# The dilation-16 attention group by 16 classes of 64 tokens, in 64x64 products

## The chip, the cores and the metric

The kernel runs on one core of a Trainium2 chip. The metric is the device time of one execution in microseconds, the median over the runs shown. Inside the core, TensorE (PE) multiplies matrices and writes to PSUM, PEld is its weight load, VectorE (DVE), ScalarE (ACT) and GpSimd (POOL) work element by element, and SyncE (SP) and POOL issue DMAs between HBM and SBUF.

## The reference, cut to what matters

A residual stream of 1024 tokens by 1024 channels goes through two layers. Layer 0 is a gated short convolution (a product 1024 to 8192 columns, a width-3 convolution, a product 2048 to 1024). Layer 1 is dilated attention:

```python
proj = h @ w_in                                   # 3 groups x (q, k, v) x 16 heads x 64, and z
for g, (window, dilation) in enumerate(((128, 1), (512, 4), (2048, 16))):
    q = rms_norm(qkv[:, :, g, 0], q_gain[g]); k = rms_norm(qkv[:, :, g, 1], k_gain[g])
    # query t sees keys t - dilation*j, j = 0..128, causal, plus a bias of the distance
    o, l = dilated_group_attention(q, k, v, bias_g, window, dilation)
alpha = softmax(stack(lses)); o = sum(alpha * outs)   # the groups are merged by their denominators
y = o * silu(z); x = x + y @ w_out
```

With dilation 16 the 1024 tokens fall into 16 residue classes of 64 tokens. Within a class, attention is plain causal attention over 64 positions; tokens of different classes don't see each other.

## The kernel before, in words

All tensors are float32, and channels lie on partitions (two heads of 64 on 128 partitions). The program has three stages in time.

**Convolution** (to about 790 us) and **projections** (to about 1624 us). Both multiply by a Strassen scheme in three-term split products of 128x128 by 512 (lines L301 to L304), so PE does one of these every 0.23 us. The order of PE's instructions is written out by hand; the other engines' order comes from a planner that estimates times. Weights are loaded by SP, mixed on POOL (L276) and split on ACT and DVE (L164, L165). The projections come in pairs of 128 columns, one pair for q and k (`qk`), then one of v for two units (`v`), then the gate (`z`). A unit is a pair of heads `hp` (8 of them) and a group `g` (0, 1, 2 for dilation 1, 4, 16).

For a `qk` pair, `norm` computes the RMS norm two pairs later: for each half `hf` of the tokens and each of q and k, DVE multiplies the raw product by the gain and the row factor (L711) and writes it into a scratch half tile with the tokens sorted by residue class (1, 4 or 8 classes; `c`), and POOL stores each half tile to HBM (`qkd`, L716). For a `v` pair, `got` scales the product into scratch (POOL at L683 for three of four pieces, DVE at L681 for the fourth); `turn` then transposes it in 128-token blocks (PE, L727; `blk` picks the tokens of a block, for dilation 16 every eighth token) and stores it (`vd`, L733).

**Attention** (1624 to 1972 us). All engines' orders are written by hand: `attention(hp, g)` makes steps, and a loop takes one step per iteration: part A of step k, part C of step k-4, then the later parts of the merging, then part B of step k-2, and then, in iterations 33 to 48, 53 to 68 and from 73 on, one piece of the output projection ("dense", L1091 to L1093). A unit of group 0 or 1 has 4 steps, a unit of group 2 has 2, so a head pair takes 10 iterations.

For dilation 16 the kernel treats the tokens as 8 classes of dilation 8, each one block of 128 tokens. Half of each 128x128 score block belongs to the other residue modulo 16, and the bias table masks it.
- A: 4 blocks x 2 heads of 64x128 products `q x k` into two score banks (L902); then, per block and head, DVE adds the bias and takes the row maximum (L919, with a read of the accumulator), and ACT takes the exponential and its row sum (L922).
- B: PE transposes the 8 blocks (L929), and ACT or DVE copies them out of PSUM (L859, L857).
- C: per block, head and query half, a product of V (128 keys) with the transposed weights (L942), written with a step of 8 tokens into two output banks; after the second step `finish` copies them to SBUF (DVE, L959).

Merging of the three groups: `store` writes the row maxima and sums of groups 0 and 1 to HBM (`nld`) and, at group 2, loads them back (`ml`, L965, on POOL's queue). `weights` (DVE, L979 and on) and `shares` (to L997) make the shares; `store_shares` (L1000) writes them and `spread` (L1005) loads them back broadcast. For the last head pair `spread_last` does this with PE transposes instead (L1040: 24 for each token half), and `last` multiplies (L1047).

SP loads q and k (L831), v (L839), bias tables (L872) and others some iterations ahead. DMA waits are in order on each queue.

## Time and profile before

| what | value |
|---|---|
| median of 3 runs | 1978.61 us (1975.02 to 1979.72) |
| the profiled execution | 1973.57 us, span 1971.8 us |
| PE busy | 1925.4 us, 98% of the span |
| DVE busy | 1493.2 us, 76% |
| ACT busy | 903.5 us, 46% |
| POOL busy | 880.9 us, 45% |
| chain that ended last | PE 78%, DVE 12%, issue 4%, DMA 4%, ACT 3% |

Busy times are shares of the whole span, over stages with different limits. A busy PE is one with a matmul in flight; several small ones can be in flight at once, so what a stretch of small products costs is read from the start of one run of instructions to the start of the next.

### The profile page before, as it was taken

What the parts mean: (1) busy time and instruction counts of PE and PEld (TensorE: products, weight loads), DVE (VectorE), ACT (ScalarE), POOL (GpSimd) and SP (SyncE); (2) the same over time, 40 slices, a digit from 0 to 9 for tenths busy, and PEclk for the clock granted to TensorE, in tenths of its full rate; (3) what the DMA queues carried; (4) which work ended last, traced back from release to release, by engine and by line L of the source; (5) the groups of instructions that cost most, each with busy time, mean ns of one, the idle gap of its engine ahead of it and who ended that gap; (6) DMA issues with size and microseconds to landing.
All of it is one profiled execution on the core that took longest, in us unless ns stands there. A gap on an engine that the chain in (4) does not pass through costs nothing.

```text
span 1971.8 us, 30228 instructions
## 1 busy us (share of the span) xinstructions
PE 1925.4 (98%) x10654; PEld 1566.2 (79%) x10654; DVE 1493.2 (76%) x2754; ACT 903.5 (46%) x2042; POOL 880.9 (45%) x800
## 2 busy tenths in 40 slices
PE   8999999999999999999999999999999999899998
PEld 6888888888888888878888888788888876677777
DVE  7866666666566555788889689968998866788886
ACT  6433333333334454444333443434334339877781
POOL 0366657666665211344445445444444451323230
PEclk9999999999999999999999999999999999999999
DMA  5312232222224575423233233324333257978752
GB/s 195 118 58 91 83 107 76 96 89 84 91 70 152 185 239 167 133 76 112 103 118 118 76 118 106 118 76 128 87 107 107 98 180 248 258 222 225 203 158 86
DMA packets 116807, 254.28 MB, mean 129 GB/s; under 512 B 15822, under 2 KB 22718, under 8 KB 116656
## 3 DMA queue, kind: packets, MB, share of 16 engines
q1 hardware_dynamic: 93024, 177.42, 28.3%
q0 software_dynamic: 23632, 74.95, 12.6%
q8 instruction: 83, 1.36, 0.3%
q14 instruction: 68, 0.56, 0.1%
HBM read 193.05 MB, written 67.64 MB: 132 GB/s over the span
## 4 chain that ended last, share of the span: by engine, by line
PE 78%; DVE 12%; issue 4%; DMA 4%; ACT 3%; SPq 0%; POOL 0%; DVEq 0%; POOLq 0%; ACTq 0%
PE pp L301 18%; PE pp L304 18%; PE pp L303 18%; PE pp L552 3%; PE pp L553 3%; PE pp L551 3%; DVE ws L165 2%; PE pt L929 2%; DVE blkc L711 1%; PE pp L374 1%; PE po L948 1%; PE pp L375 1%; PE pp L376 1%; ACT xs L922 1%; DMA wraw<-in_wo 1%
## 5 line engine op out<-in xcount | busy, mean ns | idle before, releaser
L165 DVE TENSOR_TENSOR ws<-wr,ws 128x512 fp32r<-128x512 f32 x284 | 281.2, 992 | 115.5 <-ACT ws L164 113.9
L164 ACT ACTIVATE ws<-wr 128x512 fp32r<-128x512 f32 x284 | 178.3, 630 | 361.3 <-PE pp L304 238.9
L164 ACT ACTIVATE ws<-sr 128x512 fp32r<-128x512 f32 x272 | 169.9, 629 | 294.0 <-PE pp L304 244.1
L276 POOL TENSOR_TENSOR sr<-wr 128x512 f32<-128x512 f32 x136 | 185.0, 1360 | 261.1 <-DMA wr<-in_wqk 74.8
L165 DVE TENSOR_TENSOR ws<-sr,ws 128x512 fp32r<-128x512 f32 x272 | 228.7, 848 | 74.0 <-ACT ws L164 71.4
L313 DVE TENSOR_TENSOR f<-pp,f 128x512 f32<-128x512 f32 x204 | 139.7, 685 | 91.3 <-PE pp L304 84.3
L922 ACT ACTIVATE xs<-xs,nl 128x128 f32<-128x128 f32 (+1 forms) x384 | 167.9, 440 | 49.6 <-DVE nl L919 48.0
L309 ACT ACTIVATE f<-pp 128x512 f32<-128x512 f32 x228 | 132.5, 581 | 26.3 <-POOL blkc L683 12.2
L716 POOL DMA_DIRECT2D qkd<-blkc x96 | 68.0, 716 | 133.8 <-DVE blkc L711 126.4
L919 DVE CUSTOM_DVE_ANT_0 xs<-ps,bt 128x128 f32<-128x128 f32 (+1 forms) x384 | 110.7, 347 | 21.3 <-PE ps L907 14.3
L674 ACT ACTIVATE f<-f 128x512 f32<-128x512 f32 x96 | 60.7, 632 | 142.0 <-DVE f L313 104.8
L276 POOL TENSOR_TENSOR sr<-wr,sr 128x512 f32<-128x512 f32 x68 | 88.8, 1305 | 67.2 <-issue 43.9
L301 PE MATMUL pp<-blkg,ws 128*128 128x512 f32 x272 | 107.0, 393 | 3.4 <-ACT f L309 3.4
L301 PE MATMUL pp<-blkf,ws 128*128 128x512 f32 x272 | 108.5, 399 | 0.7 <-ACT f L309 0.7
L301 PE MATMUL pp<-blka,ws 128*128 128x512 f32 x272 | 107.1, 394 | 0.7 <-ACT f L309 0.7
L301 PE MATMUL pp<-blkb,ws 128*128 128x512 f32 x272 | 107.4, 395 | 0.0
L301 PE MATMUL pp<-blkd,ws 128*128 128x512 f32 x272 | 107.0, 393 | 0.0
L304 PE MATMUL pp<-blkf,ws 128*128 128x512 f32 x272 | 106.3, 391 | 0.0
L304 PE MATMUL pp<-blkd,ws 128*128 128x512 f32 x272 | 106.0, 390 | 0.0
L304 PE MATMUL pp<-blka,ws 128*128 128x512 f32 x272 | 106.0, 390 | 0.0
L304 PE MATMUL pp<-blkb,ws 128*128 128x512 f32 x272 | 106.0, 390 | 0.0
L303 PE MATMUL pp<-blkg,ws 128*128 128x512 f32 x272 | 105.9, 389 | 0.0
(335 smaller groups left out, 5356.6 us busy)
## 6 DMA issues: line engine op xcount, KB each, us to landing
wr<-in_conv_w_in SPq DMA_DIRECT2D x128, 256.0 KB, 3.1
wr<-in_wqk SPq DMA_DIRECT2D x96, 256.0 KB, 3.1
qkd<-blkc POOLq DMA_DIRECT2D x96, 256.0 KB, 3.2
qk<-qkd SPq DMA_DIRECT2D x48, 512.0 KB, 6.5
wr<-in_conv_w_out SPq DMA_DIRECT2D x64, 256.0 KB, 3.1
f<-in_x SPq DMA_DIRECT2D x48, 256.0 KB, 4.1
wr<-in_wv SPq DMA_DIRECT2D x48, 256.0 KB, 3.0
vd<-f POOLq DMA_DIRECT2D x48, 256.0 KB, 2.5
```

What stands on the lines that cost most here:

```text
L164: nc.scalar.activation(t[:, 0], src, AF.Copy)
L165: nc.vector.tensor_tensor(t[:, 1], src, t[:, 0].bitcast(F32), op=OP.subtract)
L276: nc.gpsimd.tensor_tensor(t, x, y, op=op)
L301: nc.tensor.matmul(ps, w[:, 0, ws], b[:, k, 0], start=new and k == 0, stop=False, skip_group_check=not new)
L303: nc.tensor.matmul(ps, w[:, 0, ws], b[:, k, 1], start=False, stop=False, skip_group_check=not new)
L304: nc.tensor.matmul(ps, w[:, 1, ws], b[:, k, 0], start=False, stop=end and k == 3, skip_group_check=not new)
L309: nc.scalar.activation(t, ps, AF.Copy)
L313: nc.vector.tensor_tensor(m, ps, m, op=OP.add)
L674: nc.scalar.activation(sq, t, AF.Square)
L716: nc.gpsimd.dma_start(qkd[hp, g, which].rearrange("p (c s) -> p c s", c=c) [:, :, hf * m:(hf + 1) * m], o.rearrange("p (c s) -> p c s", c=c))
L919: nc.vector.tensor_tensor_reduce(out=x, in0=ps[s][:, x0:x0 + nk].rearrange("p a b -> p (a b)"), in1=u["bt"][s][:, bs], op0=OP.add, op1=OP. ...
L922: nc.scalar.activation(x, x, AF.Exp, bias=nm, scale=-1.0, accum_out=L)
```

## The change

Group 2 is treated as 16 classes of 64 tokens. Scores and values become 64x64 products: each uses one quarter of PE (64 rows by 64 columns), and four consecutive ones use the four quarters. A step of group 2 takes 8 classes: in A 16 products write scores of 128 partitions (two classes) by 64 keys, so DVE and ACT run over 64 columns in place of 128; in B two classes side by side share one transpose, 4 in place of 8; in C 16 products of 64x64.

What goes with it: `norm` sorts group 2 into 16 classes and writes whole 1024-token tiles, stored by one DMA for q and one for k (2 per unit in place of 4); `got` writes group 2's v sorted by class; `turn` then reads contiguous blocks; the bias of group 2 is loaded as 64 rows twice; `finish` sorts the output back to token order while it copies; `ml` and `store_shares` become two DMAs of 64 partitions each; `spread_last` uses products with a 64-column selection of the identity in place of transposes; the bias table of group 2 has no masked half.

```diff
@@ got, kind v
-                        if ps is not None:
-                            nc.vector.tensor_tensor(vt, ps, R1[:, cs], op=OP.mult)
-                        else:
-                            nc.gpsimd.tensor_tensor(vt, t, R1[:, cs], op=OP.mult)
+                        eng, t, r = (nc.vector, ps, R1[:, cs]) if ps is not None else (nc.gpsimd, t, R1[:, cs])
+                        if units[p[1] + col][1] == 2:
+                            vt = spare()[:, col * S:col * S + S].rearrange("p (r x i) -> p i x r", r=4, x=4)
+                            vt = vt[:, hf * 32:hf * 32 + 32]
+                            t, r = (y.rearrange("p (i x r) -> p i x r", x=4, r=4) for y in (t, r))
+                        eng.tensor_tensor(vt, t, r, op=OP.mult)
@@ norm
-                            nc.gpsimd.dma_start(qkd[hp, g, which].rearrange("p (c s) -> p c s", c=c)
-                                                [:, :, hf * m:(hf + 1) * m], o.rearrange("p (c s) -> p c s", c=c))
+                    for which in range(2):
+                        nc.gpsimd.dma_start(qkd[hp, g, which], out_tile(which))
@@ prefetch
+                    if g == 2:
+                        for hs in (lo, up):
+                            nc.sync.dma_start(b0[hs, :64], rows[:64, :64])
@@ A
+                    for n, j in enumerate(js) if g == 2 else ():
+                        for h in range(2):
+                            cols = slice((8 * h + j) * 64, (8 * h + j) * 64 + 64)
+                            for s, hs in enumerate((lo, up)):
+                                nc.tensor.matmul(flat[s][64 * h:64 * h + 64, n * 64:n * 64 + 64], q[hs, cols],
+                                                 k[hs, cols], start=True, stop=True)
+                        todo.append((slice(n * 64, n * 64 + 64), j, slice(0, 64)))
+                        if n % 2 == 0:
+                            c.append((n // 2, j, 2 * j, True, True))
@@ C
-                            if g == 2:
-                                for q in range(2):
-                                    nc.tensor.matmul(u["po", q][hs].rearrange("p (i r) -> p r i", r=8)[:, j],
-                                                     V[:, vb, hs], pts[s][:, i, q * 64:q * 64 + 64], start=f, stop=l)
+                        for a in range(2) if g == 2 else ():
+                            for s, hs in enumerate((lo, up)):
+                                for h in range(2):
+                                    rows = slice(64 * h, 64 * h + 64)
+                                    nc.tensor.matmul(u["po", h][hs, (vb + a) * 64:(vb + a) * 64 + 64],
+                                                     V[rows, vb + a, hs], pts[s][rows, i, 64 * a:64 * a + 64],
+                                                     start=True, stop=True)
@@ finish
+                if g == 2:
+                    nc.vector.tensor_copy(O[hp, g].rearrange("p (i a h r) -> p h r a i", a=2, h=2, r=4)[:, q],
+                                          u["po", q].rearrange("p (r a i) -> p r a i", r=4, a=2))
@@ store, store_shares
-                    nc.gpsimd.dma_start(u["ml"], nld[hp].rearrange("(i r) g e -> i r g e", r=8))
+                    for a, hs in enumerate((lo, up)):
+                        nc.gpsimd.dma_start(u["ml"][hs], nld[hp].rearrange("(i a r) g e -> a i r g e", a=2, r=8)[a])
-                nc.gpsimd.dma_start(fd[hp].rearrange("w s (i r) -> i w s r", r=8), u["fo"])
+                for a, hs in enumerate((lo, up)):
+                    nc.gpsimd.dma_start(fd[hp].rearrange("w s (i a r) -> a i w s r", a=2, r=8)[a], u["fo"][hs])
@@ spread_last
-                        nc.tensor.transpose(fb.rearrange("p (i r) -> p r i", r=8)[:, r],
-                                            u["wide", w][hs, r * P:r * P + P], ident[hs, hs])
+                        nc.tensor.matmul(fb.rearrange("p (i a r) -> p r a i", a=2, r=8)[:, r],
+                                         u["wide", w][:, r * P:r * P + P], mine, start=True, stop=True)
```

## Rows read from the trace of the kernel before

**Rows 1.** The head of the profile's page: the span, and of each engine the busy time, its share of the span and the number of instructions.
```profile
span 1971.8 us, 30228 instructions
PE 1925.4 (98%) x10654; PEld 1566.2 (79%) x10654; DVE 1493.2 (76%) x2754; ACT 903.5 (46%) x2042; POOL 880.9 (45%) x800
```

**Rows 2.** Busy time by stretch. The columns are the stretch (us), its length, the busy time of PE, PEld, DVE, ACT and POOL with the number of instructions, the granted TensorE clock, the share of time that the DMA engines were busy, and GB/s.
```profile
1200.00:1400.00 200.00, 197.48 (x894) 162.47 (x893) 167.65 (x246) 80.81 (x140) 96.74 (x91) 1.00 0.33 104
...
1674.00:1685.00 11.00, 9.19 (x109) 7.09 (x106) 10.68 (x53) 10.64 (x48) 3.08 (x2) 1.00 1.08 229
...
1706.00:1717.00 11.00, 7.38 (x92) 5.75 (x84) 9.96 (x46) 10.55 (x49) 3.07 (x2) 0.94 1.08 235
...
1758.00:1774.00 16.00, 16.00 (x206) 12.21 (x205) 14.24 (x50) 11.64 (x42) 3.84 (x4) 1.00 0.42 129
...
1814.00:1855.00 41.00, 41.00 (x444) 31.71 (x443) 34.34 (x136) 30.12 (x118) 11.65 (x13) 1.00 0.73 197
...
1798.00:1813.00 15.00, 12.11 (x186) 8.80 (x185) 14.64 (x52) 13.70 (x46) 3.78 (x3) 1.00 0.31 99
```

**Rows 3.** Waits between 900 and 1620 us (who waited for whom, us in total, times, longest), and the instructions of line L683 (duration in ns, least, median, most).
```profile
PE pp L301 <- ACT f L309: 4.1, 11, 1.3
...
ACT f L309 <- POOL blkc L683: 10.0, 9, 1.5
...
L683 POOL TENSOR_TENSOR blkc<-f,sqacc x36: 1282/1528/1797, 862.3 to 1599.6; 128x512 f32<-128x512 f32 x36
```

**Rows 4.** Groups of instructions by line and shape from 1480 us to the end: busy us, mean ns of one, and the idle time before them with what ended it.
```profile
L922 ACT ACTIVATE xs<-xs,nl 128x256 f32<-128x256 f32 x176 | 87.3, 498 | 29.5 <-DVE nl L919 29.1
L929 PE MATMUL pt<-ident,xs 128*128 128x128 f32 x560 | 83.3, 286 | 15.9 <-ACT pts L859 11.4 <-DVE pts L857 3.1 <-ACT xs L922 0.7
L922 ACT ACTIVATE xs<-xs,nl 128x128 f32<-128x128 f32 x208 | 80.7, 390 | 20.1 <-DVE nl L919 19.0 <-ACT pts L859 1.1
...
L919 DVE CUSTOM_DVE_ANT_0 xs<-ps,bt 128x256 f32<-128x256 f32 x176 | 64.9, 420 | 12.2 <-PE ps L907 12.0
...
L859 ACT ACTIVATE pts<-pt 128x512 f32<-128x512 f32 x88 | 47.7, 579 | 2.0 <-PE pt L929 2.0
L919 DVE CUSTOM_DVE_ANT_0 xs<-ps,bt 128x128 f32<-128x128 f32 x208 | 47.6, 286 | 9.1 <-ACT xs L922 3.2 <-PE ps L902 2.3 <-PE ps L907 2.3
...
L902 PE MATMUL ps<-qk 64*128 64x128 f32 x416 | 34.4, 293 | 3.2 <-DMA qk<-qkd 3.2
...
L959 DVE COPY o<-po 128x512 f32<-128x512 f32 x48 | 32.3, 686 | 1.6 <-PE po L948 1.2 <-PE po L942 0.4
...
L942 PE MATMUL po<-pts,V 128*64 128x64 f32 x512 | 20.2, 232 | 0.7 <-DVE o L959 0.7
...
L859 ACT ACTIVATE pts<-pt 128x256 f32<-128x256 f32 x24 | 7.9, 362 | 0.0
```

**Rows 5.** PE's own order of time between 1828 and 1850 us, like instructions merged: start us, busy us, line and shape, count. What a run costs PE is the distance to the start of the next.
```profile
1828.39 0.66 PE L929 MATMUL pt<-ident,xs 128*128 128x128 f32 x4
1828.80 0.47 PE L1091 MATMUL pd<-y,y 128*128 128x512 f32 x1
...
1830.36 1.16 PE L902 MATMUL ps<-qk 64*128 64x128 f32 x16
1831.45 0.66 PE L948 MATMUL po<-pts,V 128*64 128x128 f32 x8
1832.04 1.09 PE L929 MATMUL pt<-ident,xs 128*128 128x128 f32 x8
1832.89 0.48 PE L1091 MATMUL pd<-y,y 128*128 128x512 f32 x1
...
1847.97 1.20 PE L942 MATMUL po<-pts,V 128*64 128x64 f32 x32
1849.11 0.87 PE L929 MATMUL pt<-ident,xs 128*128 128x128 f32 x6
```

**Rows 6.** The 64x64 products of groups 0 and 1 that already use four quarters: all of them (duration in ns, least, median, most), and the last four of one run in order of time.
```profile
L907 PE MATMUL ps<-qk x704: 322/323/580, 1624.7 to 1907.9; 64*64 64x192 f32 x176
...
1685.76 0.34 PE L907 MATMUL ps<-qk 64*64 64x192 f32 x4
```

**Rows 7.** The order of time at four places in the first 100 us of attention, with the idle time before and what ended it.
```profile
1653.96 0.56 POOL L965 DMA_DIRECT2D ml<-nld  x1 [6.10 <-DMA nld<-nl]
...
1659.56 0.18 DVE L979 TENSOR_TENSOR mx<-ml 128x16 f32<-128x16 f32 x1 [0.78 <-DMA ml<-nld]
...
1691.40 0.17 DVE L979 TENSOR_TENSOR mx<-ml 128x16 f32<-128x16 f32 x1 [1.93 <-DMA ml<-nld]
...
1717.45 0.80 PE L902 MATMUL ps<-qk 64*128 64x128 f32 x4 [3.23 <-DMA qk<-qkd]
```

**Rows 8.** DVE's order of time in `norm`: four writes sorted into 8 classes (group 2), and two unsorted ones (group 0).
```profile
927.26 4.05 DVE L711 SCALAR_TENSOR_TENSOR blkc<-f,gain 128x512 f32<-128x512 f32 x4
...
949.78 1.41 DVE L711 SCALAR_TENSOR_TENSOR blkc<-f,gain 128x512 f32<-128x512 f32 x2
```

**Rows 9.** The order of time where the last head pair's second half is spread and multiplied.
```profile
1946.30 1.70 PE L1040 MATMUL ps<-ident,qk 64*128 64x64 f32 x24
1947.05 1.88 DVE L1047 TENSOR_TENSOR o<-o,ps 128x512 f32<-128x512 f32 x3 [3.35 <-PE ps L1040]
...
1949.59 0.50 PE L1092 MATMUL pt<-qk,y 128*128 128x512 f32 x1 [1.15 <-DVE qk L1056]
```

More of the change, by code (lines that the diff above doesn't have):

```diff
@@ L645, in trunk @@
             space = {}
-            outs = [0]
             def spare():
@@ L651, in spare, with out_tile @@
                 return space["t"]
-            def out_tile():
-                outs[0] += 1
-                o = 2 * S + outs[0] % 4 * HALF
-                return spare()[:, o:o + HALF]
+            def out_tile(which):
+                return spare()[:, 2 * S + which * S:3 * S + which * S]
             due = {}
@@ L915, in A @@
                         xs.append(ap.tile([P, 4, P], F32, name="xs", tag="xs", bufs=6))
-                        for x0, nk, j, bs in todo:
+                        for cols, j, bs in todo:
                             nm, L = nml(j, s)
-                            x = xs[s][:, x0:x0 + nk].rearrange("p a b -> p (a b)")
-                            nc.vector.tensor_tensor_reduce(out=x, in0=ps[s][:, x0:x0 + nk].rearrange("p a b -> p (a b)"),
+                            x = xs[s].rearrange("p a b -> p (a b)")[:, cols]
+                            nc.vector.tensor_tensor_reduce(out=x, in0=flat[s][:, cols],
                                                            in1=u["bt"][s][:, bs], op0=OP.add, op1=OP.min, scale=-1.0,
@@ L958, in finish @@
                     O[hp, g] = ap.tile([P, S], F32, name="o", tag="o", bufs=5)
-                nc.vector.tensor_copy(O[hp, g][:, half(q)], u["po", q])
+                if g == 2:
+                    nc.vector.tensor_copy(O[hp, g].rearrange("p (i a h r) -> p h r a i", a=2, h=2, r=4)[:, q],
+                                          u["po", q].rearrange("p (r a i) -> p r a i", r=4, a=2))
+                else:
+                    nc.vector.tensor_copy(O[hp, g][:, half(q)], u["po", q])
             def store():
@@ L1059, in attention @@
             for q in range(2):
-                for js in ([[4 * q, 4 * q + 1, 4 * q + 2, 4 * q + 3]] if g == 2 else
+                for js in ([[2 * q, 2 * q + 4, 2 * q + 1, 2 * q + 5]] if g == 2 else
                            [[4 * q, 4 * q + 1], [4 * q + 2, 4 * q + 3]]):
```

40 lines of the change are left out of this document (21 added, 19 removed).

## The prediction

> **What bounds the kernel now.** I read the head of the page first [rows 1]: PE is busy 98% of the span, so a change counts where it shortens PE's order or a wait of PE's. Next the busy times by stretch [rows 2]. In the projections PE is busy 197.5 of 200 us; what the change moves there can hardly gain, only add to PE's few waits. Attention has three regimes. In its first 100 us (1674 to 1685, 1706 to 1717) PE is idle a sixth to a third of the time, ACT and DVE are nearly always busy, and the DMA engines are saturated (the share there is 1.08). Where the output projection lies beside attention (1758 to 1774, 1814 to 1855) PE is busy without a gap, DVE some 84 to 89%. In the gap between two such stretches (1798 to 1813) DVE is busy 14.64 of 15 us and PE only 12.1. So the same edit is worth three different things, by place.
>
> **The change part by part.** I call the 8 units of group 2 by their head pairs, 0 to 7.
>
> *PE, per step.* B: 4 transposes in place of 8. With dense work behind, 8 take 0.85 us from start to start and 4 take 0.41 [rows 5]: -0.44 us. A: now 16 instructions, 1.09 us to the next start; C: now 32, 1.14 us [rows 5]. A product takes two instructions (256 products of C in the code, x512 in the row [rows 4]). After, A and C have 32 each, in rounds of four quarters. The price is not in the trace, so bounds. Upper: C's present spacing with two in parallel, (1.20 - 0.22)/31 = 0.032 us each, so 1.14 us again. Lower: rounds of four in the time that C's rounds of two take now (0.063 us): 8 rounds, 0.51, plus the 0.13 by which C's 1.14 exceeds its 16 rounds: 0.64 us. That four can run together is in the rows: a round of L907 is busy 0.34 us where one instruction takes 0.323, so its four starts lie within 0.02 us [rows 6]. But those rounds come 0.16 us apart, so no row shows rounds this dense, and I take the middle, 0.89: A -0.20, C -0.25. A step is then worth 0.89 us of PE (0.40 to 1.39), a unit 1.8.
>
> The Trainium skill speaks against the lower bound: "TensorE: Matmul & The Clock Gate", section "Wait — 56ns, not 53.3ns?", says that start-to-start never drops below about 25 ns however small the product is. Four starts within 0.02 us [rows 6] don't agree with it for a burst; for a sustained run no row decides. By that rule A and C would take 32 x 0.025 + 0.13 = 0.93 us each (an estimate), and the sum below would lose some 0.6 us.
>
> *ACT and DVE.* An exponential over 256 columns takes 498 ns and one over 128 takes 390 [rows 4]; 64 fewer columns then save 54 ns, 16 per unit: 0.86 us. The copies after the transposes go from 512 to 256 columns, 579 to 362 ns [rows 4], three of four on ACT: 0.65 us. DVE's bias step goes from 420 ns at 256 and 286 at 128 columns by another 67 ns: 1.07 us per unit; `finish` gets slower: its writes step by 16 tokens. The nearest row is L711: four sorted writes take 4.05 us, two unsorted 1.41 [rows 8], so 1.01 against 0.70 us for one, and I add that 0.31 to each of two copies of 686 ns [rows 4] (bounds 0 and twice that): +0.6 per unit, which leaves DVE 0.7 ahead with its share of the copies (0.2).
>
> *Where it counts.* Units 3 and 5 lie wholly beside dense work, where PE has no gap: DVE's gain of 0.7 and ACT's of 1.5 come along, so PE's 1.8 us is the gain: -3.6 for both. Units 4 and 6 fall into the gap where DVE is the bound: their second step's eight bias steps (0.54) and one copy (0.2) come off DVE, and the one A and the one C that lie beside dense work off PE (0.45): -1.2 each, -2.4. The slower `finish` lands after the gap, where DVE has room.
>
> Units 0 to 2: ACT is the busiest engine and would gain 1.5 us per unit, but DMA landings pace this stretch. In unit 0 DVE waits 0.78 us for `ml`, in unit 1 1.93 us, and PE 3.23 us for q and k after unit 2 [rows 7]; those three times hang on DMAs issued before group 2's steps or queued behind saturated engines. What is saved before such a wait makes it longer. DVE's wait for `ml` holds back the next step's bias work, hence ACT and PE. And `ml` becomes two DMAs: POOL takes 0.56 us for one [rows 7], so the second lands about that much later, twice on the path: +1.1. After the wait at 1717 the rest of unit 2 (C twice, its copies, less `finish`) gives -0.6. Together +0.5 (from -3.5, if ACT decides after all, to +3).
>
> *The last unit and the end.* PE gains in A of the two steps, beside dense work (-0.4), and in B and C on the final chain (2 x 0.69): -1.8; ACT's shorter exponentials of the last step there another 0.4. `spread_last` turns 24 transposes, one instruction each, into 24 products of two. 24 now take (1.70 - 0.22)/23 = 0.064 us each [rows 9]; 48 then 3.1 us, +1.5 per half (bounds 0 and, at the transposes' 0.85/8 = 0.106 [rows 5], +3.5). In the second half DVE's third multiplication (a third of 1.88 us [rows 9]) ends 1.4 us later, and PE already waits 1.15 us for that chain [rows 9]: +1.4. In the first half PE has other work behind, but DVE's two slower copies (+0.6) and the later spread push the chain by +0.8. Sum: 0 (from -2 to +3).
>
> *Projections.* Group 2's v is written in steps, 12 pieces on POOL and 4 on DVE. PE waits 11 times, 4.1 us, for ACT's copy, which in turn waits 9 times, 10 us, for POOL's L683 [rows 3]. In 4 of the 12 v pairs the piece that ACT waits for is one of group 2's. No row shows POOL writing in steps. If it costs what DVE pays, 0.31 us [rows 8], and all of it passes on to PE in those 4, with a little for DVE's own four: +1.5 (from -1, if half as many store issues make POOL prompter, to +6, if a stepped write takes twice L683's 1.53 us [rows 3]). The store by whole tiles waits longer for its second half, but the tiles are next written a `qk` pair later, and POOL's queue carries half as many issues; `turn` and `norm` keep their instruction counts: nothing.
>
> SP issues two more, smaller bias loads per unit, and less data in all: nothing, but for the saturated stretch, where it is in the +0.5.
>
> *Sum*: -3.6 - 2.4 + 0.5 + 0 + 1.5 = -4.0 us. The profiled execution took 1973.57 us, 5.0 below the median of the runs shown; it becomes 1969.6, and by the median of 1978.6 the forecast is 1974.6.
>
> **The rivals.**
>
> R1, faster: rounds of four run at 0.063 us, and ACT, not the DMA, decides in units 0 to 2. Then A and C take 0.64 us, units 3 and 5 give 2.8 each, units 4 and 6 1.7, units 0 to 2 1.2 each, the end 1.0 and the projections cost nothing: -13.6, 1965. For it: the four starts of [rows 6], and ACT busy 10.64 of 11 us [rows 2]. Against: DMA share 1.08 in the same rows, and three waits that end with a landing [rows 7].
>
> R2, no gain: POOL's stepped writes take twice as long and the delay passes through ACT to PE: the projections cost +6, so +0.5 in all, 1979. For it: the wait chain exists [rows 3]. Against: PE's 11 waits come to 4.1 us in 720, so most of POOL's delay is absorbed now.
>
> R3, slower: the quarters don't overlap when K is 64 and only 64 columns move, and each instruction takes the 0.064 us of a lone 64-column one [rows 9]. A and C take 2.05 + 0.13 = 2.2 us each: +1.1 each per step, and a unit loses 2 x (2.2 - 0.44) = 3.5 us where it gained 1.8. Over units 3 to 7 that is 17.5, over units 0 to 2 some 5 more, the spread's 2.2 less ACT's 0.4 and the projections' 1.5 as before: +26, about 2004. The point from which the change loses on PE: 32 + 32 instructions must fit into 1.09 + 1.14 + 0.44 - 0.26 = 2.41 us, 0.038 each. Against it: C now runs at 0.032 with only two halves.
>
> **How the numbers follow.** Forecast 0.60, its own range 1970 to 1979; R1 0.20; R2 0.13; R3 0.07. A measurement tells 0.3% (5.9 us) from no change: faster is below 1972.7, slower above 1984.5. Faster: R1's 0.20 and a third of the forecast's 0.60, 0.40. Slower: R3's 0.07 and somewhat less than half of R2's, 0.12. The same: the rest, 0.48. The range leaves out half of R1, R3 and the far end of R2: 1965 to 1982.
>
> **What would show it.** B by 4 instructions at 0.41 us beside dense work; A and C at 0.89 us: near 0.64 speaks for R1, above 1.2 for R3. The stretch from 1814 that is 41 us now [rows 2] shorter by 1.8. DVE's L979 in units 0 and 1 still ended by the landing of `ml`, with a longer wait, and PE's wait for q and k after unit 2 still there: if these are gone, my reading of the first 100 us is wrong. L683 of group 2 longer than that of the others, and PE's waits for L309 above 4.1 us for the projections. L1040 at 3.1 us in place of 1.7. `finish` at about 1.0 us. I am wrong if the projections' end moves by over 3 us, or if the first 100 us of attention gain over 2 us.

## The result and the profile after

The changed kernel takes 1984.3 us (median of 6, 1983.06 to 1989.96), the kernel before 1978.5 in the same comparison: ratio 1.0037, 95% interval 1.0023 to 1.0052. That is 5.8 us slower, where 4.0 faster was forecast; it lies above the range (1965 to 1982) and above the 1979 of rival R2. The profiled execution took 1984.99 us, near its median; that of the kernel before [rows 1] took 1.5 us less than the fastest of the runs beside it, so the two spans differ by 11.4 us where the medians differ by 5.8. A second trace of the kernel before, taken later (`b2_again` below), is needed to read the first one.

I cut each trace at five marks: PE's transposes after its wait near 846 us, the first score product, and the first of the two copies with which `finish` ends group 2 (L959 before, L977 after) in units 2, 6 and 7. `g1_both` and `i5_sums` are experiments.

| stage, us | before | before again | after | g1_both | i5_sums |
|---|---|---|---|---|---|
| to PE's work after 846 | 846.3 | 846.4 | 846.4 | 847.4 | 848.1 |
| from there to the first score product | 778.0 | 780.9 | 781.3 | 780.7 | 783.2 |
| to unit 2's copy | 109.8 | 114.1 | 118.6 | 114.0 | 117.4 |
| to unit 6's copy | 159.9 | 159.9 | 155.0 | 153.7 | 156.0 |
| to unit 7's copy | 37.7 | 36.9 | 35.4 | 35.5 | 35.6 |
| to the end | 40.1 | 41.7 | 46.4 | 42.6 | 40.5 |

The gain is where it was forecast, in units 3 to 6: -4.8 us. Unit 7's stage gains another 1.5 to 2.3. It is lost at both ends of attention: +4.5 to +8.8 in units 0 to 2 and +4.7 to +6.3 from unit 7's copy to the end. The head of the page of the kernel after, and its groups by line and shape:

```profile
span 1983.2 us, 30581 instructions
PE 1921.2 (97%) x10894; PEld 1559.8 (79%) x10894; DVE 1490.1 (75%) x2754; ACT 892.9 (45%) x2042; POOL 846.4 (43%) x767
```
```profile
L937 ACT ACTIVATE xs<-xs,nl 128x64 f32<-128x64 f32 x128 | 42.7, 336 | 12.3 <-DVE nl L934 12.3
L934 DVE CUSTOM_DVE_ANT_0 xs<-ps,bt 128x64 f32<-128x64 f32 x128 | 19.8, 220 | 0.8 <-ACT xs L937 0.8
L977 DVE COPY o<-po 128x512 f32<-128x512 f32 x16 | 15.3, 1032 | 0.0
L958 PE MATMUL po<-pts,V 64*64 64x64 f32 x512 | 14.6, 243 | 1.8 <-DVE o L980 1.8
L903 PE MATMUL ps<-qk 64*64 64x64 f32 x512 | 11.8, 224 | 1.9 <-DVE nl L934 1.9
L1063 PE MATMUL ps<-ident,qk 128*128 128x64 f32 x96 | 11.0, 275 | 0.0
```

DVE's bias step, the exponentials and `finish` [rows 4] have the durations forecast: 220 ns (286 - 67 = 219), 336 (390 - 54), 1032 (some 1.0 us). PE's own order, merged as in [rows 5], gives the price of the quarters:

```profile
1840.01 0.69 PE L903 MATMUL ps<-qk 64*64 64x64 f32 x32
1840.64 0.66 PE L965 MATMUL po<-pts,V 128*64 128x128 f32 x8
...
1855.70 0.64 PE L958 MATMUL po<-pts,V 64*64 64x64 f32 x32
1856.84 0.88 PE L944 MATMUL pt<-ident,xs 128*128 128x128 f32 x6 [0.50 <-ACT pts L861]
...
1859.73 0.64 PE L958 MATMUL po<-pts,V 64*64 64x64 f32 x32
1860.31 1.09 PE L944 MATMUL pt<-ident,xs 128*128 128x128 f32 x8
```

A takes 0.63 us to the next start where it took 1.09. The unit's second C takes 0.58 where it took 1.14; the first takes 1.14 still, because PE now waits 0.50 us behind it for ACT's copy. So the quarters run at R1's bound (0.64), not at the 0.89 that I took. Now the two ends. First unit 0: the waits of the kernel after in attention, and POOL's order there.

```profile
PE ps L922 <- DVE nl L934: 11.0, 7, 4.3
POOL fb L1028 <- issue: 15.5, 4, 4.0
DVE o L1070 <- PE ps L1063: 8.5, 5, 4.4
DVE mx L1001 <- DMA ml<-nld: 5.9, 2, 5.0
```
```profile
1654.00 0.71 POOL L992 DMA_DIRECT2D nld<-nl  x1 [7.46 <-ACT xs L937]
1661.30 1.09 POOL L987 DMA_DIRECT2D ml<-nld  x2 [6.59 <-DMA nld<-nl]
1670.66 1.38 POOL L1023 DMA_DIRECT2D fd<-fo  x2 [8.27 <-DVE fo L1019]
1674.46 2.11 POOL L1028 DMA_DIRECT2D fb<-fd  x4 [2.42 <-DMA fd<-fo]
```

DVE's wait for `ml` in unit 0 went from 0.78 us [rows 7] to 5.0, and PE waits behind it (4.3 at most). The first of these lines goes out 2.61 us after the exponential that it waits for, 0.29 in the kernel before. POOL's same store and load in the second trace before:

```profile
1651.26 0.71 POOL L970 DMA_DIRECT2D nld<-nl  x1 [5.14 <-ACT pts L859]
1658.53 0.56 POOL L965 DMA_DIRECT2D ml<-nld  x1 [6.57 <-DMA nld<-nl]
```

Counted from the first score product (1627.29 us there, 1627.71 after the change), the store goes out at 24.0 us before and at 26.3 after, the load of `ml` at 31.2 and 33.6, DVE's first use of it comes at 36.7 and 39.5, and unit 0's copy at 41.6 and 44.4. So the late store passes down the chain and is most of unit 0's +2.8 us. Unit 1 takes 34.4 us in both traces, unit 2 38.1 before and 39.8 after.

Second, the end: where 24 transposes took 1.70 us [rows 9] for a half, the 48 instructions of a half now take 5.57, and DVE's multiplications wait for each bank in turn.

```profile
1935.72 0.69 PE L958 MATMUL po<-pts,V 64*64 64x64 f32 x32
1936.34 5.57 PE L1063 MATMUL ps<-ident,qk 128*128 128x64 f32 x48
```
```profile
1938.76 0.69 DVE L1070 TENSOR_TENSOR o<-o,ps 128x512 f32<-128x512 f32 x1
1940.16 0.69 DVE L1070 TENSOR_TENSOR o<-o,ps 128x512 f32<-128x512 f32 x1 [0.72 <-PE ps L1063]
1941.95 0.69 DVE L1070 TENSOR_TENSOR o<-o,ps 128x512 f32<-128x512 f32 x1 [1.10 <-PE ps L1063]
```

### The profile page after: what moved, and what is told of

Same layout as the page of the kernel before. It is cut to its first block, busy times and chain, and to the rows that moved or that the text cites. A ratio compares the mean times of both kernels' runs of the same rounds, so it can differ in the third digit from the quotient of the medians.

```text
span 1983.2 us, 30581 instructions
## 1 busy us (share of the span) xinstructions
PE 1921.2 (97%) x10894; PEld 1559.8 (79%) x10894; DVE 1490.1 (75%) x2754; ACT 892.9 (45%) x2042; POOL 846.4 (43%) x767
## 4 chain that ended last, share of the span: by engine, by line
PE 77%; DVE 12%; issue 4%; DMA 3%; ACT 3%; POOL 1%; SPq 0%; DVEq 0%; POOLq 0%; ACTq 0%
PE pp L301 18%; PE pp L304 18%; PE pp L303 18%; PE pp L552 3%; PE pp L553 3%; PE pp L551 3%; DVE ws L165 2%; PE pt L944 2%; PE po L965 2%; DVE blkc L716 1%; PE pp L374 1%; PE pp L375 1%; PE pp L376 1%; ACT xs L937 1%; PE ps L922 1%
## 5 line engine op out<-in xcount | busy, mean ns | idle before, releaser
L165 DVE TENSOR_TENSOR ws<-wr,ws 128x512 fp32r<-128x512 f32 x284 | 276.6, 976 | 120.3 <-ACT ws L164 118.8
L937 ACT ACTIVATE xs<-xs,nl 128x256 f32<-128x256 f32 (+2 forms) x384 | 161.2, 422 | 58.6 <-DVE nl L934 55.4
L309 ACT ACTIVATE f<-pp 128x512 f32<-128x512 f32 x228 | 132.7, 582 | 29.6 <-POOL blkc L682 14.1
L934 DVE CUSTOM_DVE_ANT_0 xs<-ps,bt 128x256 f32<-128x256 f32 (+2 forms) x384 | 102.4, 325 | 22.5 <-PE ps L922 10.5
L301 PE MATMUL pp<-blkg,ws 128*128 128x512 f32 x272 | 107.0, 394 | 3.9 <-ACT f L309 3.9
L301 PE MATMUL pp<-blkb,ws 128*128 128x512 f32 x272 | 108.1, 397 | 0.0
L303 PE MATMUL pp<-blkb,ws 128*128 128x512 f32 x272 | 106.7, 392 | 0.0
L304 PE MATMUL pp<-blkb,ws 128*128 128x512 f32 x272 | 106.6, 392 | 0.0
L276 POOL TENSOR_TENSOR sr<-sr,wr 128x512 f32<-128x512 f32 x68 | 104.4, 1535 | 4.9
```

What stands on the lines that cost most here:

```text
L165: nc.vector.tensor_tensor(t[:, 1], src, t[:, 0].bitcast(F32), op=OP.subtract)
L276: nc.gpsimd.tensor_tensor(t, x, y, op=op)
L301: nc.tensor.matmul(ps, w[:, 0, ws], b[:, k, 0], start=new and k == 0, stop=False, skip_group_check=not new)
L303: nc.tensor.matmul(ps, w[:, 0, ws], b[:, k, 1], start=False, stop=False, skip_group_check=not new)
L304: nc.tensor.matmul(ps, w[:, 1, ws], b[:, k, 0], start=False, stop=end and k == 3, skip_group_check=not new)
L309: nc.scalar.activation(t, ps, AF.Copy)
```

## The experiments

Medians are of 4 to 12 executions (`b2_again` is one); the kernel before, beside them, took 1977.8, 1979.0, 1979.3, 1978.9 and 1979.2 us in the five batches. The changed kernel ran in none of these, so a difference from its 1984.3 us goes across batches; the ratios to the kernel before, with their intervals, are the safer measure (1.0037 for the changed kernel). Diffs are against the changed kernel (or against the kernel before, for names that begin with b, and `h2_bfill`).

**The end and the DMAs, each undone.** `e1_tail`:
```
-  mine = ident.rearrange("p (a h i) -> p h a i", a=2, h=2)[:, hf]
-  nc.tensor.matmul(..., u["wide", w][:, r * P:r * P + P], mine, start=True, stop=True)
+  nc.tensor.transpose(..., u["wide", w][hs, r * P:r * P + P], ident[hs, hs])
```


> The changed kernel with spread_last as it was before: 24 transposes of 64 rows per half in place of 24 products over all 128 rows (the shares then come out at the wrong tokens; the work is that of before). Theory T: the 48 instructions of a half take 5.57 us in the changed kernel's trace and 24 transposes took 1.71, and PE is busy without a gap there, so BOTH halves count: the group goes back to 1.7 us, the time from the last unit's second stepped copy to the end goes from 46.4 back to about 40 us, and the median falls by 6 to 8 us, to 1976 to 1978. Rival (the prediction's own reading, that PE's part of the first half is hidden): only the second half counts, -3.9 us, 1980.5.

1980.8 us (ratio 1.0014, 1.0003 to 1.0025). A half takes 1.7 us again, so 7.6 us left PE's order; but the last stage only went from 46.4 to 42.6. The rival's size came, for a reason that neither theory gave: without the long products PE waits 2.15 us for DVE's sums in the first half (0.39 in the changed kernel), and in this execution seven products after that wait start 0.43 us apart in place of 0.23 (the granted clock from 1943 to 1946 us is 0.61):

```profile
1942.97 0.50 PE L1114 MATMUL pd<-y,y 128*128 128x512 f32 x1 [2.15 <-DVE acc L1150]
...
1944.27 0.63 PE L1115 MATMUL pd<-y,y 128*128 128x512 f32 x1
1944.70 0.63 PE L1116 MATMUL pd<-y,y 128*128 128x512 f32 x1
```

The seven cost 1.4 us. The spread had hidden a wait of DVE's. The slow products don't belong to that wait: in `g1_both` those behind the same 2.15 us start 0.23 us apart, and seven slow ones stand behind a later wait of 1.15 us. All eight traces with the short spread (24 transposes a half) have such a stretch at the end and the kernel after has none; of the two traces before, the first has none (40.1 us) and the second has one (41.7); `f1_pad` below, with the long spread, has one too (48.0). Like with like the change costs the last stage 6.3 us (46.4 against 40.1, 48.0 against 41.7), and the short spread gives back 5.4 (48.0 to 42.6).

`e2_onedma` stores and loads ml and fd by one DMA each, as before:
```
-  for a, hs in enumerate((lo, up)):
-      nc.gpsimd.dma_start(u["ml"][hs], nld[hp].rearrange("(i a r) g e -> a i r g e", a=2, r=8)[a])
+  nc.gpsimd.dma_start(u["ml"], nld[hp].rearrange("(i r) g e -> i r g e", r=8))
...
-  for a, hs in enumerate((lo, up)):
-      nc.gpsimd.dma_start(fd[hp].rearrange("w s (i a r) -> a i w s r", a=2, r=8)[a], u["fo"][hs])
+  nc.gpsimd.dma_start(fd[hp].rearrange("w s (i r) -> i w s r", r=8), u["fo"])
```

> The changed kernel with ml loaded by one DMA and fd stored by one, in the layout of before (the maxima and shares then belong to the wrong tokens; bytes are the same, and the number of DMAs is that of before). Theory M1 (the two DMAs are what made the first 110 us of attention longer): from the first score product to the first product of the output projection goes from 117.8 back to about 110 us, the median falls by 6 to 8, to 1977. Theory M2 (the two DMAs cost only the second one's 0.5 us of issue and 0.9 us of landing, twice per unit; the rest is that PE and ACT now come sooner to a chain of landings that takes as long as before): DVE's wait for ml in unit 0 goes from 5.0 to some 4 us, and the median falls by 1 to 2.5, to 1982 to 1983.

1981.9 (1.0024, 1.0014 to 1.0035). DVE's wait for `ml` in unit 0 stays at 5.1 us, so that wait doesn't come from the two DMAs; but the stretch from the first score product to the output projection's first falls from 117.8 to 114.5.

`g1_both` (both edits together):

> The changed kernel with the old spread_last and with ml and fd by one DMA each (both leave the shares at the wrong tokens). Alone they gave 1980.8 (-3.5) and 1981.9 (-2.4). If the two are separate terms of the loss they add: 1978 to 1979, the time of the kernel before, and what is left of the quarters' gain is then eaten in the first 110 us by something else. If they overlap: 1980 or more.

1976.0 (0.9985, 0.9975 to 0.9994): faster than the kernel before. The two terms are together 8.3 us by the medians (some 10 by the ratios), and the rest of the change gains 3.3. That is less than was forecast for it: without the 1.1 and 2.2 us that it charged for the two terms itself, the forecast is -7.3. Unit 0 is still 1.5 us longer here than in the second trace before.

`j1_fd` undoes fd alone, ml stays at two:
```
-  for a, hs in enumerate((lo, up)):
-      nc.gpsimd.dma_start(fd[hp].rearrange("w s (i a r) -> a i w s r", a=2, r=8)[a], u["fo"][hs])
+  nc.gpsimd.dma_start(fd[hp].rearrange("w s (p r) -> p w s r", r=8), u["fo"])
...
+  u["fb", w].rearrange("p (a i r) -> p i a r", a=2, r=8)   # in scale()
```


> The changed kernel with fd written by one DMA, in the order of the partitions, and DVE's scaling reading the spread shares in that order (runs of 8); the output is the reference's. ml stays at two DMAs. Theory: the two terms are equal, so half of e2's -2.4 comes back: 1982.5 to 1983.5, with fd issued by one instruction of some 0.85 us and the spread 1 us sooner after it. If DVE's scaling in runs of 8 is dearer than its 1.22 us, by more than 0.3, the gain is lost: 1984 or more.

1983.3 (1.0028, 1.0018 to 1.0038). In the trace the same stretch is 114.45 us, as in `e2_onedma`, with ml still doubled. This stretch scatters between executions (it is 114.8 in `f1_pad`, where both are doubled), but a part of it doesn't: unit 2's copy comes 36.3 to 37.8 us after unit 1's in all seven runs with one fd store (from `e2_onedma` to `i5_sums`), 38.3 to 40.5 in the changed kernel and the six others with two (the runs that move the store left out), and 36.7 and 38.1 in the two traces before. So fd's term is some 2 us, in unit 2. In unit 1 the spread is issued 2.7 us after the store in each of those seven runs, and 5.2 to 5.9 us after the first of two. POOL's order there in the kernel after, then in `j1_fd`:

```profile
1703.92 1.38 POOL L1023 DMA_DIRECT2D fd<-fo  x2 [5.63 <-DVE fo L1019]
1709.19 2.10 POOL L1028 DMA_DIRECT2D fb<-fd  x4 [3.90 <-issue]
```
```profile
1702.56 0.86 POOL L1022 DMA_DIRECT2D fd<-fo  x1 [5.97 <-DVE fo L1019]
1705.31 2.06 POOL L1027 DMA_DIRECT2D fb<-fd  x4 [1.88 <-DMA fd<-fo]
```

The second of the two stores lands 4.1 us after its issue, the single one 2.5. Groups of the kernel after, then of `j1_fd`:

```profile
L1028 POOL DMA_DIRECT2D fb<-fd x28 | 14.7, 534 | 26.2 <-issue 15.5 <-DMA fd<-fo 10.7
L1023 POOL DMA_DIRECT2D fd<-fo x14 | 9.6, 694 | 55.9 <-DVE fo L1019 55.9
```
```profile
L1031 DVE TENSOR_TENSOR o<-o,fb 128x1024 f32<-128x1024 f32 x14 | 17.1, 1219 | 0.9 <-DMA fb<-fd 0.9
L1027 POOL DMA_DIRECT2D fb<-fd x28 | 14.5, 524 | 16.5 <-DMA fd<-fo 14.4 <-PE ps L917 2.1
L1022 POOL DMA_DIRECT2D fd<-fo x7 | 6.1, 866 | 51.9 <-DVE fo L1019 51.9
```

POOL's idle time before the spread is 26.2 us in the one and 16.5 in the other, over 7 units: it holds six issues, and the next unit's stores of maxima, behind the landing of the later half. DVE's scaling in runs of 8 costs what it did (1219 and 1220 ns). The median moved by 1.0 us only, though, within its interval: the size rests on the traces.

`b2_again`, the kernel before once more, one execution:

> The kernel before once more, for a second trace. If its first trace is typical: first score product to the first product of the output projection 109 us within 1, unit 0's second copy 40.2 us after the first score product, POOL's second store of group 1's maxima 0.29 us after its last exponential. If that trace was a lucky one: 112 us or more, and then the loss of the first 110 us is smaller than the two traces say.

One execution, 1981.6 us, span 1979.8. The stretch from the first score product to the output projection's first is 113.2 us (109.0 in the first trace), to unit 0's copy 41.55 (40.15), the projections 780.9: the first trace was a lucky one in two stages, by 7 us in all; the other stages agree within 0.1 to 1.6. This execution in turn lies 2.7 us above its median. The spans before and after differ by 11.4 us with the first trace and by 3.4 with the second, the medians by 5.8. Part of the difference between the two traces before is the clock after PE's wait at 846 us, before anything the change touches. Windows of the kernel before, of it again, and after (the window and its length; busy us of PE, PEld, DVE, ACT and POOL, with instructions; then the granted clock as a share of full speed, the DMA share and GB/s):

```profile
846.00:850.00 4.00, 3.73 (x19) 3.18 (x20) 1.64 (x5) 0.85 (x2) 1.29 (x1) 1.00 0.04 6
```
```profile
846.00:850.00 4.00, 3.57 (x11) 3.02 (x12) 1.49 (x4) 1.14 (x3) 1.29 (x1) 0.58 0.04 4
```
```profile
846.00:850.00 4.00, 3.58 (x12) 2.96 (x13) 1.48 (x4) 0.60 (x1) 1.27 (x1) 0.62 0.06 4
```

With the granted clock at its lower level, 1.2 GHz (0.50 from 847.5 to 849.7 us in the second trace before, 0.52 from 846.8 to 850 after), 6 to 8 products take 0.2 us more each: 1.2 to 1.6 us that one execution has and another has not.

**The wait for `ml`.** `e3_late` and `b3_late`:
```
-  todo = [(LB, weights), (3, shares), (3, store_shares), (3, lambda: spread(2)),
+  todo = [(3, weights), (5, shares), (5, store_shares), (5, lambda: spread(2)),
```


> The changed kernel with the weights one step later and the shares, their store and the spread two steps later (scale and add one step later; gate unmoved). Theory M2: DVE waits in its own order for the landing of ml (5.0 us in unit 0, 0.9 in unit 1) and keeps the next bias steps, the exponentials and PE behind it; with a step more in between the wait in unit 0 falls under 1 us, the stretch from the first score product to the first product of the output projection goes from 117.8 to 111 to 114 us, and the median falls by 3 to 6, to 1978 to 1981. Rival D (landings of q, k and v under saturated DMA engines pace this stretch): PE then waits for another landing, the stretch stays within 1.5 us of 117.8, and the median within 1.5 of 1984.

> The kernel before with the same move of weights, shares, store and spread. Its DVE waits were 0.78 us in unit 0 and 1.93 in unit 1. Theory M2: these go, and at most 1 to 2.5 us with them: 1976 to 1977.5. Rival D: PE's wait of 3.2 us for q and k after unit 2 takes up what is saved: 1978.5, no change. If it gains as much as the changed kernel does, the chain has nothing to do with the change.

2002.1 and 2000.1: 18 and 22 us slower, so neither theory. fd's store and the six spread issues fell behind the next unit's stores of maxima in POOL's queue. Waits of `b3_late`:

```profile
DVE o L1008 <- DMA fb<-fd: 7.9, 3, 3.3
DVE sz L1014 <- POOL o L1011: 7.9, 2, 4.5
```

`f5_late1` moves them by one step:
```
-  todo = [(LB, weights), (3, shares), (3, store_shares), (3, lambda: spread(2)),
-          (3, lambda: spread(1)), (3, lambda: spread(0)), (8, lambda: scale(2)),
+  todo = [(3, weights), (LC, shares), (LC, store_shares), (LC, lambda: spread(2)),
+          (LC, lambda: spread(1)), (LC, lambda: spread(0)), (9, lambda: scale(2)),
```

> The changed kernel with weights and shares, their store and the spread one step later each (weights after the next step's scores and values, the rest a step behind, ahead of the next unit's first store of maxima on POOL), first scale one step later, gate unmoved. The move by two steps cost 18 us in both kernels because fd's store and the spread fell behind the next unit's stores in POOL's queue. Theory M2 (DVE's wait for ml's landing in units 0 and 1 costs what it lasts): the wait in unit 0 falls from 5.0 to under 2 us, the stretch from the first score product to the output projection's first from 117.8 to 113 to 115, median 1980.5 to 1982.5. Rival D (what is gained there is lost at a later landing, fd's or fb's): stretch 117 to 119 and median 1984 or more.

1996.8, so D's side, and worse than D expected: the wait in unit 0 is still 3.9 us, and the first score product to the output projection's takes 123.5 us. Unit 0 became 1.7 us shorter (42.6 against 44.4), but units 1 and 2 became 4.6 and 1.2 longer: the next unit's first store of maxima, behind the spread in POOL's queue, goes out 55.4 us after the first score product in place of 49.9. What is saved at one wait is lost at the next.

`f1_pad` puts short work on POOL ahead of attention:
```
+  pad = sm.tile([P, 1], F32, name="pad", tag="pad", bufs=1)
+  for _ in range(8):
+      nc.gpsimd.memset(pad, 0.0)
```

> The changed kernel with eight tiny memsets put into POOL's stream ahead of attention. In unit 0 of the changed kernel and of every variant of it so far POOL issues group 1's second store of maxima 26.3 us after the first score product, 2.6 us after the exponential that it waits for (0.29 us in every other unit, and in the kernel before). Theory F (the stall hangs on the place of that instruction in POOL's stream, which the change has shifted): with the stream shifted by eight the store goes out at about 24.0, ml lands 2.3 us earlier, DVE's wait for it in unit 0 falls from 5.0 to about 2.7, and the median falls by 2 to 3, to 1981.5 to 1982.5. Rival G (the delay is made by what the engines do at that moment, DVE's short bias steps above all): the store stays at 26.3 and the median within 1 of 1984.3.

1985.6, and the store still 2.61 us after its exponential: F falls. G isn't shown by that: the stall is the same within 2 ns in every trace of the changed kernel and its variants (unit 0 alone), also where needless transposes change what the engines do beside it, and absent in unit 0 of the kernel before and its variants. Why POOL waits there stays open, and no run takes it away, so that it costs unit 0 its 2.8 us rests on the chain above.

**Projections.** `e4_vplain`:
```
-  if units[p[1] + col][1] == 2:
-      vt = spare()[:, col * S:col * S + S].rearrange("p (r x i) -> p i x r", r=4, x=4)
...
```


> The changed kernel with group 2's values written unstepped in the projections (the columns then stand in the wrong order; the same bytes). Theory V: POOL's stepped multiplications are the 1.8 us by which the projections grew beside the 1.6 that the clock took after the wait at 846 us; PE's waits for ACT's copy or for L682 at 1021, 1053 and 1336 us go back to those of before, and from the clock's recovery to the first score product it is 1.5 to 2 us shorter; median 1982 to 1983. Rival: the stepped writes cost nothing on the path and the drift comes from elsewhere (one execution against another): within 0.5 us.

1984.5, and 782.05 us from 846 to the first score product: the rival. Over all traces that stage takes 778.0 to 780.9 us in kernels with the old layout (4 traces) and 779.6 to 784.5 with the new (15 besides this one); some 2 us on average, but not from POOL's stepped writes. L682 of the changed kernel, then the same line (L678) of this run (least, median and most, ns; first and last start):

```profile
L682 POOL TENSOR_TENSOR blkc<-f,sqacc x34: 1285/1311/1792, 896.7 to 1601.7; 128x512 f32<-128x512 f32 x34
```
```profile
L678 POOL TENSOR_TENSOR blkc<-f,sqacc x34: 1282/1452/1790, 895.1 to 1603.1; 128x512 f32<-128x512 f32 x34
```

These pieces come in two durations, and the 12 stepped ones have the same two: eight take 1.30 to 1.31 us and four 1.74, the plain ones mostly 1.29 or 1.73. Only DVE's four stepped pieces are dearer (1.05 to 1.06 us, the plain ones 0.65). What the 2 us are stays open; a part is that PE's transposes of v wait 0.5 us for POOL's last piece (0.7 in `e4_vplain`), and not at all before.

**The clock.** In the first 110 us the granted clock is lower after the change (0.92 in the mean, 0.95 and 0.94 in the two traces before). `h1_fill` and `h2_bfill`:
```
+  if lag == LB and k < len(steps) and not extra.get(k):
+      fill = bank("pd")
+      for _ in range(6):
+          nc.tensor.transpose(fill[:, :P], ident, ident)
```


> The changed kernel with six needless transposes (0.64 us of PE, into a bank that nobody reads) ahead of each step's own transposes, in the 41 steps that have no output projection beside them; nothing is left out. Theory C (PE, with less to do, waits longer in these steps, its granted clock falls to 1.2 GHz after the wait, and the products that follow run at half speed; the granted clock was low for 32 us of attention in the changed kernel's profile and for 16 in the kernel before): low time falls under 12 us, the first-product-to-projection stretch from 117.8 to 112 to 115, and the median falls by 3 to 6, to 1978 to 1981, although PE does 26 us more. Rival (ACT, DVE and landings pace these steps and the clock costs nothing there): the median is 1984 or more.

> The kernel before with the same six transposes per step. Theory C: its low time falls from 16 us to under 8, the gain is smaller than the changed kernel's, 0 to 2 us: 1976.5 to 1978.5; so the changed kernel comes closer to it. Rival: PE has less room in this kernel, and the needless work costs 2 us or more: 1980.5.

1988.3 (1.0047, 1.0029 to 1.0065) and 1983.5 (1.0019, 1.0011 to 1.0028). The needless work costs the kernel before 4 us; the changed kernel takes 4 us more by the median, but its interval overlaps that without (1.0023 to 1.0052). The mean granted clock of the changed kernel rose from 0.991 to 0.997. Theory C falls as a cause of the difference: the clock is up, and the changed kernel gains nothing on the kernel before. Whether the clock alone is worth anything can't be told, since the needless work delays what stands behind it. `h3_permfill` has the same lines and the shares sorted as in `f2_perm` below:

> The changed kernel with the needless transposes and with the last unit's shares permuted once, so that spread_last is 24 transposes per half (as in the run that gave a tail of 42.6 us). If theories C and T both hold the gains add: 3 to 6 from the one, 3.5 from the other, 1974 to 1978, at or below the kernel before. If only T holds: 1981.

1986.6: not even T's 1981.

**A version.** `f2_perm` sorts the last unit's shares once, so that the halves lie together:
```
+  nc.tensor.matmul(pf, u["perm"], u["fo"].rearrange("p w s r -> p (w s r)"), start=True, stop=True)
-  src = u["fo"][:, w] ...
+  src = pf[:, w] ...
```


> The changed kernel with the last unit's shares put into the order of the two halves by one product with a permutation, so that spread_last is 24 transposes of 64 rows per half again; the output is the reference's. The run with the old spread_last (wrong tokens) gave 1980.8 and a tail of 42.6 in place of 46.4 us. Theory T (two halves, of which the second counts in full and the first only where it outlasts PE's wait for DVE's sums): the permutation adds some 0.5 us on the chain of the shares; tail 42 to 43.5, median 1980 to 1982. Rival: the copies of the shares now read PSUM and the chain loses more than 2 us: 1983 or more.

1984.9, though the last stage is 42.6 us: unit 6 to unit 7 takes 37.6 in place of 35.4, over half of the 3.8 that the end gained. `i1_best` has the product further back in PE's order, and fd as in `j1_fd`:
```
-  todo = [(2, shares), (2, wide), (3, lambda: spread_last(0)), (3, lambda: last(0, 0)),
+  todo = [(2, shares), (3, lambda: spread_last(0)), (3, lambda: last(0, 0)),
+  extra[len(steps) + 1].insert(1, ending["wide"])
```

> j1_fd with the last unit's shares permuted by one product that stands behind the first half of the output projection's products there, so that PE doesn't wait for the shares; the output is the reference's. Theory: the period from unit 6 to unit 7 goes back from 37.6 to about 34.7 us, the tail stays at 42.6, and the median is 1978.5 to 1980.5, the kernel before's time. If the period stays at 37 us the loss of the permuted run was another: 1983.

1982.5, and still 37.6: not PE's order. DVE's order and ACT's there:

```profile
1929.21 1.23 DVE L1062 COPY qk<-pt 128x1024 f32<-128x1024 f32 x1 [0.58 <-PE pt L1053]
1931.53 1.23 DVE L1062 COPY qk<-pt 128x1024 f32<-128x1024 f32 x1 [1.09 <-ACT qk L1060]
```
```profile
1930.47 1.02 ACT L1060 ACTIVATE qk<-pt 128x1024 f32<-128x1024 f32 x1 [1.86 <-DVE qk L1062]
```

The three copies out of one bank wait for each other, where the copies of `fo` out of SBUF ran side by side on DVE and ACT, at 0.69 on DVE. `i3_act` puts the second stepped copy of `finish` on ACT from unit 3:
```
+  if q == 1 and hp >= 3:
+      nc.scalar.activation(to, po, AF.Copy)
```

> i1_best with the second of group 2's two stepped copies on ACT from unit 3 on. DVE is busy 19.4 of 20 us in the gaps between two pieces of the output projection and on the chain of the end: if it is the bound there, units 4 and 6 and the tail gain up to 1 us each, 1 to 3 in all: 1976 to 1979, under the kernel before. If ACT (16.5 of 20 us) is as near the bound, no change.

1982.8: no change. `i4_sbuf` copies the 48 columns into SBUF first, `i5_sums` also moves the first half's sums:
```
+  nc.vector.tensor_copy(mine.rearrange("p w s r -> p (w s r)"), pf)
...
-  (3, lambda: last(0, 1))]
+  add_sums()
+  last(0, 1)
```


> i1_best with the permuted shares copied once into SBUF (48 columns) before they are widened; the output is the reference's. If the serial copies out of PSUM were what gave the gain back, the period from unit 6 to unit 7 is 35 us in place of 37.6, the first half's transposes take 1.7 us in place of 3.5, and the median is 1978 to 1980. If not, it stays at 1982.5.

> i4_sbuf with DVE's sums of the output projection ahead of the first half's additions and gate at the end, where PE waits 1.0 us for those sums in i1_best (2.2 in the run with the old spread_last) and runs at half clock for some 1.4 us after it. If that order sets the end, the wait goes and the tail is 40 to 41.5 us in place of 42.5: median 1976.5 to 1978.5, at or under the kernel before. If the first half's gate then comes too late for the last products, the tail is as long as before: 1979 to 1980.

`i4_sbuf` 1980.6 (1.0002, 0.9989 to 1.0014): unit 6 to 7 35.6 us, as expected, the two DVE copies 0.69 us each. `i5_sums` 1978.1 (0.9989, 0.9980 to 0.9998): the wait for the sums falls from 2.4 to 0.3 us and the last stage is 40.5. PE's waits at the end, `i4_sbuf` and then `i5_sums`:

```profile
PE pd L1122 <- DVE acc L1158: 2.4, 1, 2.4
```
```profile
PE pd L1121 <- DVE acc L1157: 0.3, 1, 0.3
```

So there is a version that beats both kernels, the kernel before by 0.1% only, with an interval that just leaves out no change.

## Why the prediction was wrong, step by step

- *PE, per step.* B was right (4 transposes in 0.41 us beside the output projection). A and C were too dear: 0.63 and 0.58 us against 0.89. My lower bound, 0.64, was the right one: within a run four starts lie in 0.02 us, and a new round begins every 0.058 us (0.063 assumed). The Trainium skill, "TensorE: Matmul & The Clock Gate", section "Wait — 56ns, not 53.3ns?", would have given 32 x 0.025 = 0.80 us and more (an estimate); the trace doesn't agree with its 25 ns for products in four quarters: 0.63/32 is 0.020 with the run's end in it.
- *ACT and DVE.* Right within 4%, `finish` at 1.03 us included.
- *Units 3 to 6.* -6.0 forecast, -4.8 measured (1.4, 1.1, 1.4 and 0.9); 153.7 to 156.8 us, -3.1 to -6.2, in the other runs that don't move work there. PE's products gave more than I took, and the period less. Beside the output projection, in units 3 and 5, I took ACT's gain as coming along; PE's new wait of 0.50 us for ACT's copy, in the lines of PE's order above, shows that it doesn't. And 60 products of the output projection lie between the marks of each of these units, where 56 lay before, 1.0 us of PE; units 4 and 6 have that many fewer. In unit 4, which has the gap, DVE is busy 34 of 38.5 us, and in unit 5, beside the output projection, PE is idle 0.5 us of 38.8. Units 4 and 5 after:

```profile
1785.20:1823.70 38.50, 33.69 (x442) 24.93 (x441) 33.99 (x133) 29.86 (x116) 12.68 (x15) 1.00 0.79 216
1823.70:1862.50 38.80, 38.30 (x469) 29.40 (x468) 32.73 (x133) 27.95 (x114) 12.64 (x15) 1.00 0.68 201
```

- *Units 0 to 2.* +0.5 forecast, with +3 as the far bound; +4.5 against the second trace before, +8.8 against the first. Two steps failed. One is the price of the doubled DMAs: I charged 0.56 us of issue, twice. ml's second DMA costs nothing that a trace shows (114.5 us with one and with two). fd's costs some 2 us in unit 2, because the spread and the next stores queue behind the later landing. The other is a term that I put at nothing: unit 0's store, 2.3 us beyond the usual 0.29, was in no row, and with what hangs on it unit 0 is 2.8 us longer. My own signs went against my reading of this stretch. DVE's wait for `ml` grew in unit 0 (0.78 to 5.0 us) but fell in unit 1 (1.93 to 0.9), and PE's wait of 3.2 us for q and k after unit 2 is gone; the time lost ahead of these waits may have taken them up, which wasn't tried by itself. With one fd store it is there again, 1.6 to 2.0 us (`e2_onedma`, `g1_both`, `j1_fd`).
- *The last unit and the end.* 0 forecast, from -2 to +3; +4.0 measured like with like (unit 7's stage and the last one together 81.8 us against 77.8, and 82.6 in `f1_pad` against 78.6 where both have slow products). The step that failed is the spread's price. It was taken from transposes of 64 rows, 0.064 us each, and a product with 128 rows takes 5.57/48 = 0.116, above even the bound of 0.106 from the transposes of 128 rows: 3.9 us more per half, not 1.5. And the first half's part was hidden behind "other work": PE has no gap there, so it goes onto PE's order; only a wait that it covered, 2.15 us in place of 0.39, spares a part. The rest of the term was right: with the short spread the two stages take 77.3 us against 78.6, so -1.3, where my parts without the spread come to -1.6.
- *Projections.* +1.5 forecast, some 2 measured on average; that is luck. POOL's stepped writes cost nothing that a row shows, and PE's waits for L309 are 3.9 us (4.1 before [rows 3]). R2's mechanism didn't happen, and R3's did not either: it needed 0.038 us per instruction.
- *The base.* I worked from one execution and noted that it was 5.0 us under its median. It was so in the two stages on which most of the sum's uncertainty lay. By my sign the projections' end moved too far, by 3.4 us against the first trace; against the second it moved by 0.4.

## What to carry to other kernels

When the inner products get a new layout, price what the layout does to the seams (a store that splits in two, a selection that was a transpose) as carefully as the products; here they cost some 8 us, and all the rest gained 3. A term at the end of a kernel whose PE has no gap counts in full, unless a wait can be named that it covers. Of a waiting DMA chain, count what is queued behind its last landing on the issuing engine, not the issue alone; and take a second trace before reading a few us out of one stage.

## What the runs showed of the hardware that was not expected

- 64x64 products in four quarters of PE start 14 to 15 ns apart through a run of 32 (0.69 us busy with the last one's 0.22): four within 0.02 us, then the next four.
- An fp32 product with 128 rows of weights and only 64 moving columns takes 0.116 us per instruction, a transpose of 64 rows with 64 columns 0.064. The weight loads go with that, 192 ns in the mean against 139; but loads for the products of 64 rows in L902 take 188, and for the transposes of 128 rows in L929 143, so the rows aren't what sets them.
- PE's products start 0.43 us apart in place of 0.23 for some 3 us after some waits and not after others of the same length: after 2.15 us in `e1_tail`, not in `g1_both`; after 2.7 to 2.8 us near 846 in the kernel after and the second trace before, not in the first.
- The second of two DMA stores issued by POOL one behind the other landed 4.1 us after its issue in unit 1, a single one 2.5.
- A POOL store went out 2.61 us after the exponential it waits for, in unit 0 of the changed kernel and of each of its variants, to within 2 ns; cause not found.
